# Routing stage of a two-block transformer kernel: low halves by VectorE, adaLN products elsewhere, gates behind the slots

## The chip, the cores and the metric

The kernel runs on one core of a Trainium2 chip. The metric is device time in microseconds (us). Three runs of the kernel before took 1028.23, 1029.07 and 1030.41 us; the median is 1029.07 us. Engines are named as in the profile: PE is TensorE, DVE is VectorE, ACT is ScalarE, POOL is GpSimd, SP is SyncE, whose only work here is to issue loads.

## The reference, cut to what matters

Two transformer blocks follow each other on 256 tokens of 1024 channels. The first ends in a hierarchical mixture of experts; its routing is what the change touches. `c_2` is the condition of the second block, from which that block's shifts, scales and gates are made (adaLN).

```python
# first block, after the mixer
x = x + g1 * mix
h = _rmsnorm(x, norm2_g[l]) * (1 + sc2) + sh2
g_prob = softmax(h @ rg_w + rg_b)            # 4 groups
g_p, g_idx = top_k(g_prob, 1)
e_sel = (h @ re_w + re_b)[group g_idx]       # 8 experts of the group
e_p, e_idx = top_k(softmax(e_sel), 2); e_p = e_p / sum(e_p)
gates = g_p * e_p                            # per token, two experts
y = (silu(h[tok] @ w1[e]) * (h[tok] @ w3[e])) @ w2[e]    # all 32 experts
x = x + g2 * (sum of gate * y over the token's experts)
# second block
mod = silu(c_2) @ w_ada + b_ada              # shift1, scale1, gate1, ...
```

## The kernel before

All matrices are streamed once from HBM by SP's queue into `ring`, eight buffers of 2 MB (two pools of four), in the order of `load_list`: the mixer's matrices, `wout0` and `wout1`, then the adaLN halves `ada0s`, `ada0g`, `adag1` (each two loads, `_0` and `_4`), then for each expert `w13_e_0`, `w13_e_4` and `w2_e`, 6 MB an expert. `w2_0` goes into a buffer of its own, `px`. A load is issued when its buffer's last reader is done, and SP issues strictly in its order: a load that waits holds all behind it. Which of a pool's buffers a new tile gets, and the order of instructions on each engine, is decided when the program is laid out: a scheduler takes ready instructions by priority (`tc.high_priority` raises it), and a new tile gets the buffer that comes free first in the order so laid out. `order` rows below show what it made.

Around the change the stages are these.

- Out projection (L784 to L857, `out_products`, L788): the mixer's result times `wout0` and `wout1`. Each weight tile is split into a rounded high half (ACT, L340 or L796) and the rest (DVE, L341 or L797), and three products are made. As 256 columns of x are done, DVE adds them to `x1T` (L855), PE transposes them into `tb` in PSUM (`po`, `bank`, L833) and makes the router's sums (L843), ACT squares them (L836).
- Routing (L863 to L945): the mean square gives `r2` (POOL's power, L266), DVE makes the logits `L` (L867), picks the group (L878 to L885) and the two experts (L887 to L897) and writes the selection `Mb`; PE counts ranks from it (L904 to L908), DVE makes of them the slot `rk` of each token in each expert (L910) and the selection matrix `Q` (L1023). The gates `ga` (L918 to L928) are needed only where results are put back. Beside it the rows of x are written as high and low halves `xH`, `xL` (the tiles mixH and mixL): ACT writes the high half and a full copy `xf` out of PSUM (L943, L944), POOL subtracts (L945).
- In the same place PE makes the adaLN products (`half_products`, L246): the second half of `ada0g` and both halves of `adag1`, 48 products (96 records in the profile, as each fp32 product is two). Their condition column `csl` is a copy made by POOL (L931) in a buffer of the tag `sq7`.
- Experts: `gather` (L1039) multiplies xH and xL by `Q`, `hidden` (L1056) and `outer_products` (L1087) read the streamed weights. Expert 0's products begin while its tokens are still being gathered.

Of the kernel before, what the change touches and what calls it, by code (L numbers as in the profile page):

```python
# [7 lines left out]
F32 = mybir.dt.float32  # L8
# [4 lines left out]
AF = mybir.ActivationFunctionType  # L13
OP = mybir.AluOpType
# [102 lines left out]
def build(tc, A, dbg=None):  # L117
    nc = tc.nc
# [47 lines left out]
    def yh(name, i):  # L166

        return yx.tile([128, 1032], F32R, name=name, tag=f"{name}{i}")
# [28 lines left out]
    fr = f1.enter_context(tc.tile_pool(name="fr", bufs=1))  # L197
    ptr = early.enter_context(tc.tile_pool(name="ptr", bufs=1, space=PSUM))
# [25 lines left out]
    cs = con.tile([128, 2, 8], F32, name="cs")  # L224
# [14 lines left out]
        nc.vector.tensor_copy(R, ps)  # L239
        return R  # L240

    def half_products(ps, name, cols, k0=0, k1=8):
        for k in range(k0, k1):
            w = get(f"{name}_{k // 4 * 4}")
            for j in range(4):
                nc.tensor.matmul(ps[32 * j:32 * j + 32, :], cols[:, k:k + 1].to_broadcast([128, 32]),  # L246
                                 w[:, k % 4, 256 * j:256 * j + 256], start=(k == 0), stop=(k == 7))

    def half_t(pt, R):

# [231 lines left out]
    for k in range(8):  # L482
        for j in range(4):
            nc.tensor.matmul(pss[32 * j:32 * j + 32, :], S1[:, k:k + 1].to_broadcast([128, 32]),
                             wa[:, 1 - j // 2, k, 128 * (j % 2):128 * (j % 2) + 128],
                             start=(k == 0), stop=(k == 7))
# [15 lines left out]
    for j in range(2):  # L502
        nc.scalar.activation(sg[:, j], psg[:, 256 * j:256 * j + 256], AF.Sigmoid, bias=za[:, 2 + j:3 + j])
        nc.vector.scalar_tensor_tensor(U[:, j, 30:], psv[:, 256 * j:256 * j + 256], za[:, j:j + 1], sg[:, j],
                                       op0=OP.add, op1=OP.mult)
# [9 lines left out]
    for c in range(0, 4, 2):  # L515
        ps = bank()
# [3 lines left out]
    ps = bank()  # L520
# [7 lines left out]
    for k0, k1 in ((0, 3), (3, 6), (6, 8)):  # L528
        wH, wL = w_halves(wk[:, k0:k1, 64:328])
        for a in (1, 0):  # L530
            for n, (w_, b) in enumerate(((wH, 0), (wL, 0), (wH, 1))):
                for k in range(k0, k1):
                    nc.tensor.matmul(pss[a][:, :264], hT[b][:, k, 128 * a:128 * a + 128], w_[:, k - k0],
                                     start=(n == 0 and k == 0), stop=(n == 2 and k == 7))
# [21 lines left out]
    for a in (1, 0):  # L556
# [16 lines left out]
        for n, h in enumerate([0, 2, 1, 3, 4, 6, 5, 7]):  # L573
            if n == 0:
                nc.vector.tensor_scalar(of(acc, a), rel[h], uw[:, a, h:h + 1], 0.0, op0=OP.mult, op1=OP.add)
            elif n < 7:
                nc.vector.scalar_tensor_tensor(of(acc, a), rel[h], uw[:, a, h:h + 1], of(acc, a),
                                               op0=OP.mult, op1=OP.add)
# [16 lines left out]
    for j in range(2):  # L595
        nc.vector.scalar_tensor_tensor(cqT[:, j], psq[:, 256 * j:256 * j + 256], P("qng", j), rbq,
                                       op0=OP.mult, op1=OP.mult)
# [20 lines left out]
    for j in range(2):  # L618
        ps = bank()
# [18 lines left out]
    for c in range(0, 4, 2):  # L638
        ps = bank()
# [6 lines left out]
    for c in range(0, 4, 2):  # L646
        pss = [bank(), bank()]
        for i in range(2):
            for s in range(2):
                r = slice(64 * s, 64 * s + 64)  # L650
                nc.tensor.matmul(pss[s][:, 256 * i:256 * i + 256], wuk[r, c + i, :], qT[r, c + i, :],
                                 start=True, stop=True)
# [5 lines left out]
    ps = bank()  # L658
# [30 lines left out]
    for hh in range(2):  # L689
# [3 lines left out]
        for a in (1, 0):  # L693
            S = 128 + 128 * a
            Lg[a] = fl.tile([128, 512 + 512 * a], F32, name=f"Lg{a}").rearrange("p (h t) -> p h t", h=4)
            for h in range(0, 4, 2):
                ps = bank()
# [8 lines left out]
                for j in range(h, h + 2):  # L706
                    nc.scalar.activation(Lg[a][:, j, :S], Lg[a][:, j, :S], AF.Exp, bias=nmx[:, a, j:j + 1],
                                         scale=0.125, accum_out=sm[:, a, j:j + 1])
# [32 lines left out]
    for hh in range(2):  # L741
# [15 lines left out]
        ps = bank()  # L757
        for j in range(2):
            for s in range(2):
                h = 2 * j + s  # L760
# [5 lines left out]
    def ada_rows(name, cols, ps=None, k0=0):  # L766

        ps = ps or ptr.tile([128, 512], F32, name="mod", tag="tr")[:, :256]
        half_products(ps, name, cols, k0, 8)
        R = fo.tile([128, 512], F32, name="modR")[:, :256]  # L770
        nc.scalar.activation(R, ps, AF.Copy)
        return R
# [1 line left out]
    pt = half_t(ptr.tile([128, 512], F32, name="pa", tag="tr"), ada_rows("ada0s", cs[:, 1]))  # L774
    nc.vector.tensor_add(c42(S3), pt, c42(P("ab0", 0, 8)))
    psa = ptr.tile([128, 512], F32, name="mod", tag="tr")[:, :256]
    half_products(psa, "ada0g", cs[:, 1], 0, 4)


    w0, w1 = get("wout0"), get("wout1")  # L780
# [11 lines left out]
    for c in (6, 7, 0, 1):  # L792
        for k in (0, 2):
            v = [fl.tile([128, 256], F32R, name=n, bufs=1) for n in ("weH", "weL")]
            src = (w0 if c < 4 else w1)[:, c % 4, 128 * k:128 * k + 256]
# [8 lines left out]
    rt = ms.enter_context(tc.tile_pool(name="rt", bufs=1))  # L804
# [86 lines left out]
    for a in range(2):  # L891
# [21 lines left out]
    nc.vector.tensor_reduce(cm, prk[:, 2], AX.X, OP.max)  # L913
    nc.vector.tensor_copy(ci[:, 32:33], cm)
    nc.vector.tensor_copy(ci[:, 0:32], prk[:, 2])

    ex = rt.tile([128, 2, 8], F32, name="ex")
    nc.vector.tensor_sub(ex[:, :, 0:4], L[:, :, 0:4], gm[:, :, 0:1].to_broadcast([128, 2, 4]))  # L918
# [7 lines left out]
    nc.vector.tensor_mul(oh, oh, gt[:, :, 0:2, None].to_broadcast([128, 2, 2, 32]))  # L926
    ga = rt.tile([128, 2, 32], F32, name="ga")
    nc.vector.tensor_add(ga, oh[:, :, 0], oh[:, :, 1])  # L928
    hp.__exit__(None, None, None)
    csl = fr.tile([128, 256], F32, name="csl", tag="sq7")[:, :8]  # L930
    nc.gpsimd.tensor_copy(csl, cs[:, 1])  # L931
    R_g = ada_rows("ada0g", csl, psa, 4)
    ps1 = ptr.tile([128, 512], F32, name="mod", tag="tr")[:, :256]
    half_products(ps1, "adag1", csl)

    xH, xL = ([yh(n, a)[:, :1024].rearrange("p (k t) -> p k t", k=8) for a in range(2)]
              for n in ("mixH", "mixL"))
    for b in range(2):
        for a in range(2):
            src = tb[a, b].rearrange("t (k p) -> t k p", k=4)  # L940
            h = xH[a][:, 4 * b:4 * b + 4, :]
            xf = fr.tile([128, 4, 128], F32, name="xf", bufs=2)
            nc.scalar.activation(h, src, AF.Copy, scale=r2[:, a:a + 1])  # L943
            nc.scalar.activation(xf, src, AF.Copy, scale=r2[:, a:a + 1])  # L944
            nc.gpsimd.tensor_sub(xL[a][:, 4 * b:4 * b + 4, :], xf, h)  # L945
    fs.close()

    mo = ms.enter_context(tc.tile_pool(name="mo", bufs=1))
# [142 lines left out]
    def keep(e, ps):  # L1091
        YS[e] = late[0][:, 3072 + 256 * (e % 4):3328 + 256 * (e % 4)]
        nc.scalar.activation(YS[e], ps, AF.Copy)  # L1093
# [18 lines left out]
    nc.scalar.activation(nea, B("alog"), AF.Exp)  # L1112
    nc.gpsimd.tensor_scalar(nea, nea, -1.0, None, op0=OP.mult)

    R_1 = mo.tile([128, 256], F32, name="R_1")
    nc.scalar.activation(R_1, ps1, AF.Copy)
    slots(0)
    for k in range(0, 8, 2):
        gather(0, k, 2)
    for e in range(32):  # L1120
        if e == 28:
            most = nc.values_load(ci[0:1, 32:33], min_val=0, max_val=256)
            with tc.If(most > 32):  # L1123
                off = mo.tile([128, 1], F32, name="off")
                nc.vector.memset(off, -32.0)
                with tc.For_i(0, 4, 1) as r_:
                    with tc.If(most > 32 + 64 * r_):
                        with tc.For_i(0, 32, 1) as e_:
                            own = nc.values_load(ci[0:1, bass.ds(e_, 1)], min_val=0, max_val=256)
                            with tc.If(own > 32 + 64 * r_):  # L1130
                                overflow(e_, off)
                    nc.vector.tensor_scalar(off, off, -64.0, None, op0=OP.add)
        if e % 8 == 0 and 0 < e < 24:
            slots(e // 8 + 1)
        ps = hidden(e)
        back(e)
        if e:
            scatter(e - 1)
        if e == 8:
            pt = half_t(ptr.tile([128, 512], F32, name="pa", tag="tr"), R_g)  # L1140
            nc.vector.tensor_add(c42(G3), pt, c42(P("ab0", 8, 8)))
            nc.vector.scalar_tensor_tensor(G3, G3, 1.0, P("n1w2"), op0=OP.add, op1=OP.mult)
            nc.gpsimd.tensor_mul(G3f, G3, P("fg"))
            for j in range(4):
                nc.gpsimd.tensor_mul(abG[:, :, 8 * j:8 * j + 8], abw, G3f[:, :, None].to_broadcast([128, 8, 8]))
        if e == 10:
            pt = half_t(ptr.tile([128, 512], F32, name="pa", tag="tr"), R_1)
            nc.vector.tensor_add(c42(gt1), pt, c42(P("ab1", 0, 8)))
        if e == 12:
            pb = ptr.tile([128, 256], F32, name="pb", tag="tr")  # L1150
            for k in range(8):
                nc.tensor.matmul(pb[:, 0:8], S3[:, k:k + 1].to_broadcast([128, 128]), abw[:, k],
                                 start=(k == 0), stop=(k == 7))
            nc.vector.tensor_add(abS, pb[:, 0:8], B("dtb8"))
        if e == 6:

            nc.gpsimd.dma_start(par[:, 0:NG], A["gk"])
        aT = act(e, ps)
        if e % 2 == 0 and 0 < e < 24:
            gather(e // 8 + 1, e % 8, 2)  # L1160
        if e == 0:
            first = outer_products(0, aT)
            late.append(extra[0].tile([128, 4096], F32, name="px"))
            slots(1)
            gather(1, 0, 2)
            keep(0, first)
        else:
            keep(e, outer_products(e, aT))
        pump(min(index[f"w2_{e}"] + RING, index["w2i_k"]))
# [769 lines left out]
```

## Time and profile before

| | |
|---|---|
| median of 3 runs | 1029.07 us |
| the profiled execution | 1029.3 us |
| its span | 1027.7 us |
| PE busy | 865.2 us (84%) |
| DVE, ACT, POOL busy | 440.8, 337.9, 64.3 us |
| DMA, mean over the span | 315 GB/s, 323.80 MB |
| mean granted clock of PE | 0.898 |

The page's row of transfer rates, in 40 slices of 25.7 us, reads 353, 431, 427, 426, 414, 338, 206, 416 and then 423 to 430 until slice 25. So the loads run at some 426 GB/s nearly from the start to about 642 us, but for a dent in slices 5 and 6. [...]

### The profile page before, as it was taken

The page shows a single profiled execution, that of the slowest core. Times are in us where ns is not written, and L with a number is a line of the kernel's source. Part 1 is how long each engine was busy: PE and PEld are TensorE (multiplying, and loading weights), DVE is VectorE, ACT ScalarE, POOL GpSimd, SP SyncE. Part 2 cuts the span into 40 slices and gives each one's busy share as a digit, 9 for nine tenths or more (in the row PEclk, how much of TensorE's full clock was granted, in tenths as well). Part 3 has the DMA queues.
Part 4 walks back from the last instruction along what each step waited for, and adds up shares of the span by engine and source line. Part 5 has one row for each costly group of instructions (what it writes and reads, how often), then busy time and mean ns, then how long its engine had stood idle before and what let it go on. Part 6 is the DMA issues. An engine that isn't in the chain of part 4 may idle for free. (4 is left out here: it accounts for less than half of the span.)

```text
span 1027.7 us, 19397 instructions
## 1 busy us (share of the span) xinstructions
PE 865.2 (84%) x8134; PEld 602.9 (59%) x8135; DVE 440.8 (43%) x1051; ACT 337.9 (33%) x763; POOL 64.3 (6%) x85
## 2 busy tenths in 40 slices
PE   4999998996777787667766776989999999999996
PEld 2786676653434343233332333768989878888884
DVE  1499855321101011000000104777667476666675
ACT  4441745210100010000000004745435365555562
POOL 0000002000000000000000001342012000000000
PEclk9899999997986777787778688999999999999998
DMA  9999985999999999999999999653205546444521
GB/s 353 431 427 426 414 338 206 416 423 426 427 428 423 426 428 426 424 428 427 426 426 426 424 425 425 256 213 117 104 1 233 197 166 245 165 147 182 205 83 41
DMA packets 36125, 323.80 MB, mean 315 GB/s; under 512 B 4032, under 2 KB 4416, under 8 KB 5696
## 3 DMA queue, kind: packets, MB, share of 16 engines
q1 hardware_dynamic: 34992, 320.11, 75.5%
q10 hardware_dynamic: 864, 1.86, 0.6%
q8 instruction: 66, 1.08, 0.4%
q0 software_dynamic: 176, 0.53, 0.1%
q14 instruction: 27, 0.22, 0.1%
HBM read 321.43 MB, written 1.05 MB: 314 GB/s over the span
## 5 line engine op out<-in xcount | busy, mean ns | idle before, releaser
L341 DVE TENSOR_TENSOR wL<-ring,wH 128x512 fp32r<-128x512 f32 (+1 forms) x208 | 140.1, 680 | 93.8 <-ACT wH L340 87.1
L340 ACT ACTIVATE wH<-ring 128x512 fp32r<-128x512 f32 (+1 forms) x220 | 133.9, 614 | 123.1 <-PE gb L1242 43.0
L1087 PE MATMUL yy<-ring,aT 128*32 128x256 f32 x992 | 96.6, 554 | 34.4 <-DMA ring<-w 33.7
L1075 DVE TENSOR_TENSOR at<-sl,hh 128x128 f32<-128x128 f32 x32 | 9.2, 287 | 262.3 <-ACT sl L1073 262.3
L1056 PE MATMUL hh<-ring,px 128*32 128x256 f32 x1024 | 79.1, 445 | 23.2 <-DMA ring<-w 23.2
L1056 PE MATMUL hh<-ring,XT 128*32 128x256 f32 x1024 | 71.4, 405 | 19.2 <-DMA ring<-w 19.1
L1087 PEld LDWEIGHTS yy<-ring,aT 128*32 128x32 f32 x992 | 43.1, 150 | 75.2 <-issue 55.0
L1073 ACT ACTIVATE sl<-hh 128x128 f32<-128x128 f32 x32 | 8.9, 278 | 200.5 <-PE hh L1056 189.7
L1056 PEld LDWEIGHTS hh<-ring,px 128*32 128x32 f32 x1024 | 33.0, 124 | 63.1 <-DMA ring<-w 33.4
L1093 ACT ACTIVATE px<-yy 128x256 f32<-128x256 f32 x32 | 12.3, 384 | 153.1 <-PE yy L1087 153.1
L1056 PEld LDWEIGHTS hh<-ring,XT 128*32 128x32 f32 x1024 | 32.0, 116 | 51.4 <-DMA ring<-w 27.9
L351 PE MATMUL zb<-mixH,wH 128*128 128x258 f32 x224 | 59.2, 293 | 1.2 <-ACT wH L340 1.2
L352 PE MATMUL zb<-mixH,wL 128*128 128x258 f32 x224 | 58.7, 290 | 0.0
L1242 PE MATMUL gb<-mixH,wH 128*128 128x512 f32 x176 | 54.8, 396 | 1.6 <-DVE mixH L1697 1.4
L1242 PE MATMUL gb<-mixL,wH 128*128 128x512 f32 x176 | 54.9, 394 | 0.0
L1099 PE MATMUL acc<-MT,px 32*128 32x256 f32 x512 | 43.1, 432 | 7.4 <-PEq L1123 4.3
L351 PEld LDWEIGHTS zb<-mixH,wH 128*128 128x128 f32 x224 | 43.2, 193 | 3.9 <-issue 1.6
L352 PEld LDWEIGHTS zb<-mixH,wL 128*128 128x128 f32 x224 | 43.2, 193 | 1.5 <-issue 1.5
L1099 PEld LDWEIGHTS acc<-MT,px 32*128 32x128 f32 x512 | 26.0, 200 | 26.0 <-issue 15.0
L1069 DVE COPY MT<-tm 128x256 f32<-128x256 f32 x32 | 13.6, 424 | 64.1 <-PE tm L1067 64.1
L354 PE MATMUL zb<-mixL,wH 128*128 128x258 f32 x224 | 38.7, 291 | 0.0
L1242 PEld LDWEIGHTS gb<-mixL,wH 128*128 128x128 f32 x176 | 33.0, 188 | 7.7
(550 smaller groups left out, 1648.9 us busy)
## 6 DMA issues: line engine op xcount, KB each, us to landing
ring<-w SPq DMA_DIRECT2D x132, 1024.0 KB, 22.6
ring<-wall SPq DMA_DIRECT2D x35, 2048.0 KB, 9.8
ring<-w SPq DMA_DIRECT2D x29, 2048.0 KB, 24.6
ring<-wall SPq DMA_DIRECT2D x29, 1024.0 KB, 12.9
mx<-wall SPq DMA_DIRECT2D x8, 1024.0 KB, 5.8
px<-w SPq DMA_DIRECT2D x1, 2048.0 KB, 9.3
ring<-wall SPq DMA_DIRECT2D x1, 1600.0 KB, 25.3
ring<-wall SPq DMA_DIRECT2D x1, 1536.0 KB, 25.0
```

What stands on the lines that cost most here:

```text
L340: nc.scalar.activation(d[0], src, AF.Copy)
L341: eng.tensor_sub(d[1], src, d[0])
L351: nc.tensor.matmul(ps, wH[:, k], h[0][:, q + k], start=(q + k == 0), stop=False)
L352: nc.tensor.matmul(ps, wL[:, k], h[0][:, q + k], start=False, stop=False)
L354: nc.tensor.matmul(ps, wH[:, k], h[1][:, q + k], start=False, stop=(q + k == 7))
L1056: nc.tensor.matmul(ps[32 * j:32 * j + 32], XT[e // 8][:, k, e % 8, :], w[:, k % 4, :, 128 * j:128 * j + 128], start=(k == 0), stop=(k == 7))
L1069: nc.vector.tensor_copy(MT[e], ps)
L1075: nc.vector.tensor_mul(at, sl, ps[:, 1])
L1087: nc.tensor.matmul(ps[32 * j:32 * j + 32], aT[:, 32 * c:32 * c + 32], w[:, c, 256 * j:256 * j + 256], start=(c == 0), stop=(c == 3))
L1093: nc.scalar.activation(YS[e], ps, AF.Copy)
L1099: nc.tensor.matmul(acc[j][:, i], YS[e][r, 128 * i:128 * i + 128], MT[e][r], start=(e == 0 and i == 0), stop=(e == 31), skip_group_check=True)
L1242: nc.tensor.matmul(ps.rearrange("p (x t) -> p x t", x=2), wH[:, k], y(4 * q + k), start=(q + k == 0), stop=(4 * q + k == 7), skip_group_ch ...
```

## The change

- The low halves: ACT's full copy `xf` and POOL's subtraction go. DVE makes the low half by one instruction that reads PSUM, scales it and subtracts the high half. This now stands ahead of the gates in the code.
- The block of high priority ends behind the ranks; the gates are outside it.
- `csl` has a buffer of its own. With that, nothing holds the adaLN products back to the routing.
- Of `adag1` only the first half is multiplied ahead of the experts, and copied to `R_1` by ACT; the second half is multiplied in expert 0, behind its outer products, and added by DVE.

```diff
-    def half_products(ps, name, cols, k0=0, k1=8):
+    def half_products(ps, name, cols, k0=0, k1=8, stop=True, start=True):
...
-    half_products(psa, "ada0g", cs[:, 1], 0, 4)
+    half_products(psa, "ada0g", cs[:, 1], 0, 4, False)
...
     nc.vector.tensor_copy(ci[:, 0:32], prk[:, 2])
+    hp.__exit__(None, None, None)
+
+    xH, xL = ([yh(n, a)[:, :1024].rearrange("p (k t) -> p k t", k=8) for a in range(2)]
+              for n in ("mixH", "mixL"))
+    for b in range(2):
+        for a in range(2):
+            src = tb[a, b].rearrange("t (k p) -> t k p", k=4)
+            h = xH[a][:, 4 * b:4 * b + 4, :]
+            nc.scalar.activation(h, src, AF.Copy, scale=r2[:, a:a + 1])
+            nc.vector.scalar_tensor_tensor(xL[a][:, 4 * b:4 * b + 4, :], src, r2[:, a:a + 1], h,
+                                           op0=OP.mult, op1=OP.subtract)
...
-    hp.__exit__(None, None, None)
-    csl = fr.tile([128, 256], F32, name="csl", tag="sq7")[:, :8]
+    csl = rt.tile([128, 8], F32, name="csl")
     nc.gpsimd.tensor_copy(csl, cs[:, 1])
     R_g = ada_rows("ada0g", csl, psa, 4)
     ps1 = ptr.tile([128, 512], F32, name="mod", tag="tr")[:, :256]
-    half_products(ps1, "adag1", csl)
-
...
-            xf = fr.tile([128, 4, 128], F32, name="xf", bufs=2)
-            nc.scalar.activation(h, src, AF.Copy, scale=r2[:, a:a + 1])
-            nc.scalar.activation(xf, src, AF.Copy, scale=r2[:, a:a + 1])
-            nc.gpsimd.tensor_sub(xL[a][:, 4 * b:4 * b + 4, :], xf, h)
+    half_products(ps1, "adag1", csl, 0, 4)
+    R_1 = rt.tile([128, 256], F32, name="R_1")
+    nc.scalar.activation(R_1, ps1, AF.Copy)
...
+            ps1 = ptr.tile([128, 512], F32, name="mod", tag="tr")[:, :256]
+            half_products(ps1, "adag1", csl, 4, 8)
+            nc.vector.tensor_add(R_1, R_1, ps1)
```

What the scheduler makes of it is seen at three places. On SP, the loads behind `w2_0` (px) in the kernel before; ring_2081 is `w13_0_0`, ring_2176 `w2_1`, ring_2178 and 2181 the two loads of `w13_2`, ring_2184 `w2_2`; a wait for DVE is one for the last split of wout0 or wout1, a wait for PE one for products (a wait for DMAHW is for an older load's landing):

```order
L153 DMA px_2135<-w2 128x4096 [waits DVE_49,PE_49,DMAHW7_49,Activation_49,Pool_49]
L153 DMA ring_2081<-w13 128x2048 [waits DMAHW0_49,DVE_49]
L153 DMA ring_2081<-w13 128x2048 [waits DMAHW1_49]
L153 DMA ring_2176<-w2 128x4096 [waits DMAHW2_49,DVE_49]
L153 DMA ring_2178<-w13 128x2048 [waits DMAHW3_49,PE_49]
L153 DMA ring_2178<-w13 128x2048 [waits DMAHW4_49]
L153 DMA ring_2181<-w13 128x2048 [waits DMAHW5_49,PE_49]
L153 DMA ring_2181<-w13 128x2048 [waits DMAHW6_49]
L153 DMA ring_2184<-w2 128x4096 [waits DMAHW7_49,PE_49]
L1122 TENSOR_LOAD ci_1909 [waits PE_49,DVE_49,Activation_49,Pool_49]
L1122 ISA x2
L153 DMA ring_2186<-w13 128x2048 [waits DMAHW1_49,DMAHW0_49,PE_49]
```

In the changed kernel, on the same engine and place, ring_2057 is `w13_0_0`, ring_2172 and 2175 the loads of `w13_2`, ring_2170 `w2_1`, ring_2178 `w2_2`, ring_2258, 2261 and 2180 the loads of expert 3:

```order
L153 DMA px_2111<-w2 128x4096 [waits DVE_49,PE_49,DMAHW7_49,Activation_49,Pool_49]
L153 DMA ring_2057<-w13 128x2048 [waits DMAHW0_49,PE_49]
L153 DMA ring_2172<-w13 128x2048 [waits DMAHW2_49,PE_49]
L153 DMA ring_2175<-w13 128x2048 [waits DMAHW4_49,DVE_49]
L153 DMA ring_2170<-w2 128x4096 [waits DMAHW6_49,DVE_49]
L1121 TENSOR_LOAD ci_1909 [waits PE_49,DVE_49,Activation_49,Pool_49]
L153 DMA ring_2178<-w2 128x4096 [waits DMAHW1_49,DMAHW7_49,DMAHW0_49,PE_49]
L153 DMA ring_2258<-w13 128x2048 [waits PE_49]
L153 DMA ring_2261<-w2 128x4096 [waits DMAHW2_49,PE_49]
L153 DMA ring_2180<-w13 128x2048 [waits DMAHW3_49,PE_49]
```

(The second half of each `w13` load is left out.) Before, the first load behind px waited for wout0's last split and the three after `w2_1` for adaLN products in the routing. Now the first two wait for adaLN products, which stand earlier; the next two wait for the splits of wout0 and wout1; `w2_2` goes into the buffer of `w13_0_0` itself, and its PE wait is by its count the wait for expert 0's last hidden product from that buffer. ring_2180 takes the buffer of `adag1_4`, whose products stand behind expert 0's outer products.

On PE, the adaLN products come into the out projection (po, with the split weights weH and weL, then wH and wL); one piece of the difference:

```order
 L788 MATMUL po0_1462<-mixL_936,weH_1524 128x256
 L788 MATMUL po0_1462<-mixH_934,weL_1525 128x256
+L246 MATMUL mod_1442<-ring_1939,csl_1937 32x256 x16
 L788 MATMUL po1_1463<-mixH_934,weH_1534 128x256
 L788 MATMUL po1_1463<-mixL_936,weH_1534 128x256
```

Another 16 stand in two groups of 8 a few rows below, and the 48 that stood between the router's sums (L843) and the rank counts (L904) are gone. So PE has nothing between the router's sums and the rank counts now. On DVE, one piece of the difference at the routing; mixL is the low half, goh and em lead to the choice of experts:

```order
 L878 MAX gm<-gp 128x8 x2
+L925 SCALAR_TENSOR_TENSOR mixL<-po_1643,r_1862,mixH 128x512
 L879 MAX_INDEX gi<-gm,gp 128x8 x2
-L918 TENSOR_TENSOR ex<-L,gm 128x2x4
+L929 TENSOR_TENSOR ex<-L,gm 128x2x4
+L925 SCALAR_TENSOR_TENSOR mixL<-po_1645,r_1862,mixH 128x512
 L881 CAST gidx<-gi 128x2
+L925 SCALAR_TENSOR_TENSOR mixL<-bank,r_1862,mixH 128x512 x2
 L885 TENSOR_SCALAR goh<-kon,gidx 128x4 x2
```

The four low halves stand among the choice of the group, ahead of the choice of experts. The gates (L933 to L939 now) still stand ahead of `rk` (L910) on DVE, as they did before.

## Rows read from the trace of the kernel before

**Rows 1.** Busy us by stretch: PE, PEld, DVE, ACT, POOL; then clock, DMA share, GB/s.

```profile
150.00:160.00 10.00, 10.00 (x89) 10.00 (x88) 4.97 (x13) 5.15 (x17) 0.00 (x0) 1.00 0.11 42
160.00:170.00 10.00, 8.84 (x76) 8.43 (x75) 4.84 (x12) 3.65 (x11) 0.00 (x0) 1.00 0.29 109
170.00:180.00 10.00, 6.25 (x78) 3.25 (x81) 7.59 (x31) 6.17 (x14) 5.58 (x6) 0.83 1.01 426
180.00:190.00 10.00, 9.00 (x111) 6.26 (x107) 7.33 (x24) 3.92 (x7) 1.21 (x4) 1.00 1.02 405
190.00:200.00 10.00, 9.83 (x151) 5.80 (x139) 1.77 (x6) 1.78 (x5) 0.00 (x0) 1.00 1.00 417
200.00:640.00 440.00, 321.03 (x3646) 157.83 (x3642) 51.66 (x160) 43.61 (x126) 3.42 (x7) 0.79 1.01 426
```

**Rows 2.** Waits of PE from 200 to 640 us: total us, times, longest.

```profile
PE hh L1056 <- DMA ring<-w: 42.3, 40, 2.1
PE yy L1087 <- DMA ring<-w: 33.7, 25, 2.8
```

**Rows 3.** SP's issues in order of time, three of them: start us, us.

```profile
143.28 0.33 SPq L153 DMA_DIRECT2D px<-w  x1
...
165.91 0.33 SPq L153 DMA_DIRECT2D ring<-w  x1
...
189.68 0.34 SPq L153 DMA_DIRECT2D ring<-w  x1
```

**Rows 4.** Waits of SP from 120 to 300 us, one of them.

```profile
SPq L153 <- DVE wL L341: 22.7, 2, 22.2
```

**Rows 5.** PE in order of time at the out projection, with idle time ahead.

```profile
135.05 1.93 PE L246 MATMUL mod<-ring,cs 128*32 128x256 f32 x32
...
144.41 0.39 PE L788 MATMUL po<-mixH,weH 128*128 128x256 f32 x1 [0.39 <-ACT weH L796]
...
146.37 0.39 PE L788 MATMUL po<-mixH,wH 128*128 128x256 f32 x1 [0.77 <-ACT wH L340]
```

**Rows 6.** PE in order of time at the routing.

```profile
170.09 0.53 PE L843 MATMUL bank<-rwG,x1T 128*128 128x36 f32 x4
...
176.30 5.17 PE L246 MATMUL mod<-ring,csl 128*32 128x256 f32 x64 [2.90 <-ACT modR L771]
181.40 0.19 PE L904 MATMUL side<-Mb,trib 128*128 128x32 bf16 x1
...
182.63 0.64 PE L1039 MATMUL gx<-Q,mixH 128*128 128x256 f32 x3 [0.94 <-DVE Q L1023]
```

**Rows 7.** DVE in order of time at the routing.

```profile
172.39 0.42 DVE L867 SCALAR_TENSOR_TENSOR L<-bank,r,rb 128x36 f32<-128x36 f32 x2 [0.84 <-POOL r L266]
...
173.87 2.38 DVE L885 TENSOR_SCALAR goh<-kon,gidx 128x4 f32<-128x4 f32 x2
...
177.12 1.08 DVE L919 TENSOR_TENSOR ex<-m8e 128x2 f32<-128x2 f32 x1
...
178.63 0.22 DVE L901 TENSOR_TENSOR Mb<-oh 128x64 bf16<-128x64 f32 x1
...
178.91 0.15 DVE L922 TENSOR_REDUCE gt<-ex 128x2 f32<-128x8 f32 x1
...
179.49 0.93 DVE L925 TENSOR_TENSOR gt<-gt,ex 128x2 f32<-128x2 f32 x1
180.46 0.33 DVE L926 TENSOR_TENSOR oh<-oh,gt 128x128 f32<-128x128 f32 x1
...
181.73 0.23 DVE L910 SCALAR_TENSOR_TENSOR rk<-side,Mm 128x64 f32<-128x64 f32 x1 [0.68 <-PE side L908]
```

**Rows 8.** Groups by line and shape: busy us, mean ns.

```profile
L945 POOL TENSOR_TENSOR mixL<-xf,mixH 128x512 fp32r<-128x512 f32 x4 | 5.1, 1280 | 3.0 <-ACT xf L944 2.1 <-DVE gt L922 0.9
...
L421 DVE TENSOR_TENSOR hL<-bank,hH 128x512 fp32r<-128x512 f32 x4 | 2.5, 678 | 0.0
```

**Rows 9.** A stretch of 3 us in the routing: columns as in rows 1.

```profile
176.00:179.00 3.00, 2.70 (x28) 1.33 (x32) 2.86 (x14) 1.60 (x4) 1.50 (x2) 0.50 0.95 399
```

More of the change, by code (lines that the diff above doesn't have):

```diff
@@ L246, in half_products @@
                 nc.tensor.matmul(ps[32 * j:32 * j + 32, :], cols[:, k:k + 1].to_broadcast([128, 32]),
-                                 w[:, k % 4, 256 * j:256 * j + 256], start=(k == 0), stop=(k == 7))
+                                 w[:, k % 4, 256 * j:256 * j + 256], start=start and k == k0, stop=stop and k == k1 - 1)
     def half_t(pt, R):
@@ L768, in ada_rows @@
         ps = ps or ptr.tile([128, 512], F32, name="mod", tag="tr")[:, :256]
-        half_products(ps, name, cols, k0, 8)
+        half_products(ps, name, cols, k0, 8, start=k0 == 0)
         R = fo.tile([128, 512], F32, name="modR")[:, :256]
@@ L933, in build @@
     ps1 = ptr.tile([128, 512], F32, name="mod", tag="tr")[:, :256]
-    half_products(ps1, "adag1", csl)
[L936 to L941, printed above, removed]
-            xf = fr.tile([128, 4, 128], F32, name="xf", bufs=2)
-            nc.scalar.activation(h, src, AF.Copy, scale=r2[:, a:a + 1])
-            nc.scalar.activation(xf, src, AF.Copy, scale=r2[:, a:a + 1])
-            nc.gpsimd.tensor_sub(xL[a][:, 4 * b:4 * b + 4, :], xf, h)
+    half_products(ps1, "adag1", csl, 0, 4)
+    R_1 = rt.tile([128, 256], F32, name="R_1")
+    nc.scalar.activation(R_1, ps1, AF.Copy)
     fs.close()
@@ L1113, in build @@
     nc.gpsimd.tensor_scalar(nea, nea, -1.0, None, op0=OP.mult)
-    R_1 = mo.tile([128, 256], F32, name="R_1")
-    nc.scalar.activation(R_1, ps1, AF.Copy)
     slots(0)
```

## The prediction

> **What bounds the kernel now.** I read the transfer rates first, since a kernel that streams all its weights once can be bound by them. From 200 to 640 us the DMA share is 1.01 at 426 GB/s [rows 1], and PE, with 321 of 440 us busy, waits there for loads in 65 short waits, 76 us together [rows 2]. So in the experts' stage the loads set the end. A load's delay ahead of it is paid in full at its end, and nothing there can win it back; what follows is a chain of PE and DVE work that only shifts.
>
> Next, where did the stream stand still before 200 us? It moved 0.42 MB between 150 and 160 us and 1.09 between 160 and 170 [rows 1]. By bytes its backlog ends at about 151; the 13.57 MB from 160 to 200 (the four rates times 10 us) are 31.9 us at 426 GB/s, so it runs on as if started at 168.1. That is 17 us without loads, for one reason: SP issued px at 143.28 and the next load at 165.91 [rows 3], after 22.2 us of waiting for DVE's last split of wout0 [rows 4]. From issue to the equivalent start are 2.2 us.
>
> So this change is priced by one question: when does SP issue each load, and how many has it issued when the stream last stands still? A load of 2048 KB is 2.097 MB, 4.92 us at 426 GB/s.
>
> **The loads in the new order.** The order on SP, shown with the change, puts two loads behind px whose buffers are freed by adaLN products that now run in the out projection, from some 144 us. They go out at about 146 and 150, while px is landing, and are there by 151 + 9.8 = 161. The next two wait, as before, for the splits of wout0 and wout1, at 165.91 or a little later; they are there by 180. Then `w2_2` waits for the last hidden product of expert 0 from `w13_0_0`. Before, the load with that very wait was the one issued at 189.68 [rows 3], and it cost nothing, since five loads were still landing. Now the stream is empty when it comes. So a second hole opens, between 180 and some 193 us.
>
> The sum: before, the stream restarts with an issue at 165.91 and nothing ahead. After, it restarts with an issue at T, and four loads, 4 x 4.92 = 19.7 us, lie behind it. With the same 2.2 us to get going, the stream ends later by (T - 165.91) - 19.7. What is left is T: 189.68 and all that moves expert 0.
>
> **Out projection.** 32 products (64 records) come in. 32 records took 1.93 us [rows 5], so 3.86 us. The first 16 stand where PE waited 0.39 us for ACT; from 144.41 to 146.37 PE has six products, some 0.7 us at the spacing of those records, so 1.2 us is idle [rows 5]. Taking these gaps and some shorter ones off, I set 2.0 us; the ends are 0 (all in gaps) and 3.9 (none). DVE and ACT feed PE there and move with it. The two ACT copies of 0.4 us wait on PE and lie beside its products.
>
> **Routing, from L to rk.** Before: from 172.39 to 181.73, 9.3 us [rows 7]. POOL's four subtractions, 1.28 us each [rows 8], hold DVE up: two 4-column instructions of L885 take 2.38 us, L919 1.08 [rows 7], where instructions of such size beside them take about 0.15. With POOL's work gone 2.1 + 0.9 us go. Four low halves come onto the same engine: the nearest row is a difference of the same size out of PSUM, four in 2.5 us [rows 8], so 2.5. The first exponent sum L922, now ahead of Mb, adds 0.2. Mb is thus only 0.3 us earlier. What does go is the wait behind it: the 64 records of 176.30, which end at the rank counts' 181.40 although Mb was there from about 178.8 [rows 6, 7]. But DVE has the rest of the gates in front of rk: Mm, three steps of 0.19 (178.91 to 179.49), L926, L928, some 1.5 us in all without the 0.93 of L925. rk comes 7.5 us behind L, a gain of 1.8. The ends: 4.3 (if the halves cost nothing) and a loss of 1.2 (if DVE is held up as now by something else). ACT's four full copies `xf` lay beside DVE's work; without them nothing is gained.
>
> **PE's clock.** PE now has nothing from the router's sums, which start at 170.09 [rows 6], to the rank counts. [...]
>
> **Expert 0.** The new order reads the last of `w13_0_0` four products after a gather instead of eight: 0.2 us less. Its second `adag1` half is 32 records more, 1.9 us, and one DVE add behind the outer products. Behind it stands only the first load of expert 3, ring_2180. Three loads of 14.8 us are ahead of that on the queue, which land till some 207; the products are over at about 200. Cost nothing, unless expert 0 is 5 us later than I think.
>
> T = 189.7 + 2.0 - 1.8 + 1.0 - 0.2 = 190.7. The stream ends (190.7 - 165.9) - 19.7 = 5.1 us later, and so does the kernel. Against the profiled execution (span 1027.7, 1029.3 with what lies around it) that is 1034.4; the median is 0.2 lower, so I predict 1034.2 us.
>
> With all low ends, T is 185.2 and the kernel 0.4 us faster; with all high ends 197.2 and 11.6 slower. They will not all fall on one side: some half of either way gives 1031.2 to 1037.4.
>
> **Rivals.**
>
> - No change that can be told (within 0.2%, about 2 us): T falls between 183.6 and 187.6. The gain in routing must be 3 to 7 us larger. For it: PE's 5.17 us leave the path. Against: DVE, not PE, is then the one that rk waits for. The sum is zero at T = 185.6, which gives 1029.1; chance 0.11.
> - Faster: the two loads that are brought forward are the whole gain. This holds if `w2_2` is not held, so that the stream restarts at about 168 with the wout splits and stays full: 165.9 + 2.0 - 9.8 against 165.9, 7.8 us less, 1021.3. It decides from T = 177.5 down; between that and 183.6 the gain is smaller. Against: the gather itself began only at 182.63 [rows 6], and no reading of w13_0_0 is possible before. It could come true only if the buffer that `w2_2` waits for were another than its count says. Chance, with smaller gains, 0.08.
> - Slower by more: expert 0 runs late (cold clock through the gather, halves dearer out of PSUM), the stream also waits for `adag1_4`'s buffer behind expert 0's outer products. From T of about 195 on its products end too late for the 207 us above, and the load of ring_2180 is late as well; with T = 195 to 197 the sum gives 9.4 to 11.4 us, 1038.5 to 1040.5. Chance 0.06.
> - The change does not do what it says: the gates stay ahead of rk on DVE, as the order shows. This is in the sum already (1.5 us); were they behind, T would be some 0.8 us earlier.
>
> **How the numbers follow.** The forecast, 1031.2 to 1038, has 0.75, and all of it is slower by over 0.2%, which is about what a measurement here can tell. With the slow rival slower has 0.81, same 0.11, faster 0.08. The range 1030.5 to 1038.0 takes in the forecast and the upper edge of "no change"; it leaves out the faster cases, the rest of "no change" and the slow rival, some 0.2.
>
> **What would show it.** In rates of the changed kernel: 426 GB/s on to about 161 us, a first hole to about 169, a second from about 180 to 193, then full to about 645. On SP: two loads between 145 and 151, two near 168, `w2_2` at 190.7. On DVE: L885 near 0.3 us for two, four new instructions of some 0.65 us, rk 7.5 us behind L. On PE: the clock at 0.50 when the gather starts. I am wrong if there is no second hole, or if the stream is not full behind it.

## The result and the profile after

The changed kernel takes 1034.16 us (median of 6 runs, 1033.82 to 1036.17); the kernel before, beside it, 1028.65. The ratio is 1.0057, 95% interval 1.0044 to 1.0069: slower by 5.5 us. The profiled execution has a span of 1033.0 us, before 1027.7. The forecast was 1034.2. Two executions of the later runs, one of the kernel before (1058.37 us) and one of a variant (3252.80 us), went at a far lower mean granted clock (0.796 and 0.234) and are left out of all medians, ratios and intervals here.

The transfer rates of the changed kernel, as in [rows 1] (busy us of PE, PEld, DVE, ACT, POOL, then PE's granted clock as a share of its full speed, DMA share, GB/s):

```profile
150.00:160.00 10.00, 10.00 (x89) 10.00 (x88) 5.06 (x12) 4.75 (x14) 0.00 (x0) 1.00 0.99 407
160.00:170.00 10.00, 9.42 (x82) 9.22 (x80) 4.55 (x11) 4.88 (x15) 0.00 (x0) 1.00 0.18 66
170.00:180.00 10.00, 1.67 (x15) 1.45 (x14) 7.01 (x34) 4.08 (x10) 1.53 (x4) 0.73 0.89 375
180.00:190.00 10.00, 8.33 (x57) 6.39 (x57) 6.25 (x24) 2.68 (x5) 0.00 (x0) 0.59 0.01 2
190.00:200.00 10.00, 9.28 (x141) 5.78 (x144) 1.87 (x5) 1.50 (x4) 0.00 (x0) 1.00 0.74 279
200.00:640.00 440.00, 322.22 (x3701) 158.67 (x3693) 50.18 (x155) 40.85 (x122) 1.24 (x5) 0.80 1.01 426
```

The one hole of before has become two: 66 GB/s where the wout loads are waited for, and 2 GB/s from 180 to 190. From 200 us on the rate is 426 GB/s in both kernels, so nothing is won back. That the whole difference is a stream that ends later is seen at its end. The stretch from 640 to 720 us, first of the kernel before, then of the changed one:

```profile
640.00:720.00 80.00, 73.85 (x900) 61.96 (x901) 62.06 (x127) 44.40 (x101) 30.21 (x27) 0.96 0.53 200
```

```profile
640.00:720.00 80.00, 70.78 (x842) 57.85 (x840) 61.08 (x131) 45.65 (x104) 32.66 (x28) 0.96 0.61 229
```

29 GB/s more over 80 us are 2.3 MB that were still to come, 5.4 us at 426 GB/s.

SP's issues in the changed kernel (start us, us; beside [rows 3]):

```profile
142.61 0.33 SPq L153 DMA_DIRECT2D px<-w  x1
145.28 0.90 SPq L153 DMA_DIRECT2D ring<-w  x2
...
148.84 0.81 SPq L153 DMA_DIRECT2D ring<-w  x2
167.50 0.33 SPq L153 DMA_DIRECT2D ring<-w  x1
168.25 1.09 SPq L153 DMA_DIRECT2D ring<-w  x2
191.54 0.34 SPq L153 DMA_DIRECT2D ring<-w  x1
```

Two loads go out early, two behind the splits of wout (a load of w13 is two issues, one of w2 is one), and the next at T = 191.54. SP's waits from 120 to 300 us have the one for T in the first of these rows (total us, times, longest); the second answers to [rows 4]:

```profile
SPq L153 <- PE hh L1057: 18.6, 6, 8.3
SPq L153 <- DVE wL L341: 18.0, 2, 17.8
SPq L1121 <- DVE ci L914: 12.8, 1, 12.8
```

The third row is a wait that the prediction does not have: ahead of this load SP reads `ci`, the counts of the routing, and waits for them until 182. The wait for the hidden products follows it and ends last, so it is the one that sets T.

PE in order of time, beside [rows 5] and [rows 6]:

```profile
143.28 1.93 PE L246 MATMUL mod<-ring,csl 128*32 128x256 f32 x32
...
171.72 0.53 PE L843 MATMUL bank<-rwG,x1T 128*128 128x36 f32 x4
...
180.02 0.18 PE L904 MATMUL side<-Mb,trib 128*128 128x32 bf16 x1 [7.76 <-DVE Mb L901]
...
181.97 0.98 PE L1040 MATMUL gx<-Q,mixH 128*128 128x256 f32 x3 [1.65 <-DVE Q L1024]
...
190.84 1.50 PE L1057 MATMUL hh<-ring,XT 128*32 128x256 f32 x24
```

DVE in order of time, beside [rows 7]:

```profile
174.03 0.42 DVE L867 SCALAR_TENSOR_TENSOR L<-bank,r,rb 128x36 f32<-128x36 f32 x2 [0.83 <-POOL r L266]
174.84 0.73 DVE L925 SCALAR_TENSOR_TENSOR mixL<-po,r,mixH 128x512 fp32r<-128x512 f32 x1
...
177.88 0.35 DVE L885 TENSOR_SCALAR goh<-kon,gidx 128x4 f32<-128x4 f32 x2
...
179.74 0.22 DVE L901 TENSOR_TENSOR Mb<-oh 128x64 bf16<-128x64 f32 x1
...
181.08 0.22 DVE L910 SCALAR_TENSOR_TENSOR rk<-side,Mm 128x64 f32<-128x64 f32 x1
```

From L to rk are 7.05 us where 9.34 were [rows 7]; PE stood idle for 7.76 us up to the rank counts. And the clock, a stretch of the routing and gather beside [rows 9]:

```profile
175.00:188.00 13.00, 6.33 (x35) 5.11 (x35) 10.60 (x47) 4.27 (x8) 0.15 (x1) 0.50 0.29 124
```

The gather and the first hidden products run at the lower level, 0.50, until 188. From the gather's start to T are 9.57 us; before, at clock 1.00, 7.05 [rows 3, 6].

### The profile page after: what moved, and what is told of

It is laid out like the page before. It is cut to its first block, busy times and chain, and to the rows that moved or that the text cites. A ratio compares the mean times of both kernels' runs of the same rounds, so it can differ in the third digit from the quotient of the medians.

```text
span 1033.0 us, 19392 instructions
## 1 busy us (share of the span) xinstructions
PE 863.8 (84%) x8134; PEld 602.8 (58%) x8135; DVE 440.0 (43%) x1056; ACT 335.4 (32%) x759; POOL 59.4 (6%) x81
## 5 line engine op out<-in xcount | busy, mean ns | idle before, releaser
L1088 PE MATMUL yy<-ring,aT 128*32 128x256 f32 x992 | 94.1, 541 | 35.8 <-DMA ring<-w 35.4
```

The costliest lines, as they stand in the source:

```text
L1088: nc.tensor.matmul(ps[32 * j:32 * j + 32], aT[:, 32 * c:32 * c + 32], w[:, c, 256 * j:256 * j + 256], start=(c == 0), stop=(c == 3))
```

## Experiments

The theory is the prediction's: the kernel ends later by (T - 165.9) - 4.92 x n, T being the issue of the load that waits for expert 0's first buffer and n the loads ahead of it. This holds where the stream stands still when T comes; where it still runs, the hole before is the last one and sets the end. The main rival: something in routing itself (the low halves out of PSUM, the gates) costs the time. Diffs are against the changed kernel.

**The halves alone.** All adaLN products go back to the routing; the low halves by DVE and the gates' place stay.

```diff
-    csl = rt.tile([128, 8], F32, name="csl")
+    csl = fr.tile([128, 256], F32, name="csl", tag="sq7")[:, :8]
...
-    half_products(ps1, "adag1", csl, 0, 4)
+    half_products(ps1, "adag1", csl)
```

> The changed kernel with the adaLN products back in the routing, all 48 of them, and their buffers freed there; low halves on DVE and the gates' place stay. Theory of the holes (the end is set by when the stream of loads last restarts and how many loads lie behind that): one hole, from 151 to the wout splits at 166, five loads of 4.9 us land until 191, expert 0 frees the next buffer at 189 to 190.5, so no second hole; within 0.8 us of before, ratio 0.999 to 1.001. Rival, that the low halves on DVE or the gates cost the time: 4 to 6 us slower than before, ratio 1.004 to 1.006. Rival, that the shorter routing pays by itself: 1 to 2 us faster.

Measured: 1029.93 us, before 1029.34, ratio 0.9998 (0.9988 to 1.0007). L to rk takes 7.15 us. PE and the issues:

```profile
175.16 3.66 PE L246 MATMUL mod<-ring,csl 128*32 128x256 f32 x64 [1.74 <-ACT modR L771]
178.75 0.19 PE L904 MATMUL side<-Mb,trib 128*128 128x32 bf16 x1
180.44 0.63 PE L1038 MATMUL gx<-Q,mixH 128*128 128x256 f32 x3 [1.40 <-DVE Q L1022]
```

```profile
165.93 0.33 SPq L153 DMA_DIRECT2D ring<-w  x1
...
187.53 0.82 SPq L153 DMA_DIRECT2D ring<-w  x2
```

The buffer comes free 2.15 us earlier than before, and the time is the same: five loads behind 165.93 still land then (437 GB/s from 180 to 190 us). So with the low halves on DVE routing is shorter, they cost no time, and with one hole the shorter routing buys none.

**The adaLN products alone.** Low halves and gates as before; the products as in the changed kernel.

```diff
-            nc.vector.scalar_tensor_tensor(xL[a][:, 4 * b:4 * b + 4, :], src, r2[:, a:a + 1], h, ...)
+            nc.scalar.activation(xf, src, AF.Copy, scale=r2[:, a:a + 1])
+            nc.gpsimd.tensor_sub(xL[a][:, 4 * b:4 * b + 4, :], xf, h)
```

> The kernel before with the adaLN part of the change alone: csl in its own buffer, half of adag1 in expert 0; low halves by ACT and POOL, gates at high priority. Theory of the holes: two holes, four loads ahead of the second, expert 0 frees the next buffer at 191 to 193; 5 to 7 us slower than before, ratio 1.005 to 1.007. Rival, that the halves on DVE are what costs: ratio 0.999 to 1.002.

Measured: 1036.07, ratio 1.0064 (1.0050 to 1.0078). DVE and PE:

```profile
176.24 2.38 DVE L885 TENSOR_SCALAR goh<-kon,gidx 128x4 f32<-128x4 f32 x2
```

```profile
182.73 0.21 PE L904 MATMUL side<-Mb,trib 128*128 128x32 bf16 x1 [9.74 <-POOL trib L811]
```

Two holes again, T = 193.62. The loss is there with this part alone. L885 is back at 2.38 us: POOL's subtractions make the difference to 0.35. The rank counts wait 2 us past Mb (180.72) for `trib`, a cast that stands behind the subtractions on POOL, so T is 2.1 us later than in the changed kernel (0.7 of it because px is later in this execution).

**The second half of adag1 in routing.** It runs behind the router's sums instead of in expert 0, so that its buffer is free before the gather and n is 5.

```diff
+    csm = fr.tile([128, 256], F32, name="csm", tag="sq7")[:, :8]
+    nc.gpsimd.tensor_copy(csm, cs[:, 1])
+    half_products(ps2, "adag1", csm, 4, 8)
...
-            half_products(ps1, "adag1", csl, 4, 8)
```

> The changed kernel, but the second half of adag1 is multiplied in the routing, ahead of the rank counts, not in expert 0: its buffer comes free at about 175 and w2_2 takes it. Theory of the holes: five loads of 4.92 us lie ahead of the second hole, not four; with expert 0's first buffer free at 191 to 192 the end is 0.5 to 1.5 us later than before, so 4 to 5 us faster than the changed kernel; ratio to before 1.0005 to 1.0015. Rival, that PE's and DVE's path through the routing sets the end: as the changed kernel, ratio 1.005 to 1.006.

Measured: 1030.12, before 1029.34, ratio 1.0006 (0.9997 to 1.0015). SP:

```profile
168.03 1.75 SPq L153 DMA_DIRECT2D ring<-w  x3
175.62 0.33 SPq L153 DMA_DIRECT2D ring<-w  x1
190.98 0.81 SPq L153 DMA_DIRECT2D ring<-w  x2
```

T is within 0.6 us of the changed kernel's: the gather starts 0.86 us later (182.83), but the clock is back at 1.00 within 185 to 186 instead of at 188, and from the gather to T are 8.15 us. The time is 4.7 us below that of the changed kernel; T accounts for 0.6 of it, so the issue at 175.62 takes back some 4 of the 5.5 us. This is the run that decides for the count of loads.

**TensorE kept at work.** 24, then 11 products that nobody reads, between the sums and the rank counts (the second diff has 11 for 24).

```diff
+    for i in range(24):
+        nc.tensor.matmul(wps, r2[:, 0:1].to_broadcast([128, 128]), x1T[:, i % 8], start=True, stop=True)
```

> The changed kernel with 24 products of no use (x1T by r2, into a spare PSUM tile that nobody reads) on PE between the router's sums and the rank counts, about 5 us of work in the 7.8 us in which PE waits there. Theory that the low clock at the gather is 2 to 2.5 us of the loss: clock 1.00 from 182 on, expert 0 frees its first buffer at 189 to 189.5 instead of 191.5, so 2 to 2.5 us faster than the changed kernel, ratio to before 1.003 to 1.0035. Rival, that DVE and ACT set the pace of the gather whatever the clock: no faster than the changed kernel, 1.005 to 1.006.

Measured: 1037.79, ratio 1.0081 (1.0067 to 1.0095), outside both the expectation and its rival: 24 products were put at about 5 us and took 12.31. PE:

```profile
174.75 12.31 PE L949 MATMUL warmps<-x1T,r 128*128 128x256 f32 x48 [1.79 <-POOL r L266]
186.90 0.18 PE L904 MATMUL side<-Mb,trib 128*128 128x32 bf16 x1
188.11 0.63 PE L1043 MATMUL gx<-Q,mixH 128*128 128x256 f32 x3 [0.93 <-DVE Q L1027]
```

The rank counts came 6.9 us late, but T (195.20) only 3.7: from the gather to T are 7.09 us at clock 1.00.

> The changed kernel with 11 products added whose result nobody reads, behind the router's sums and ahead of the rank counts on TensorE. In e4_warm 24 such products took 12.3 us from 174.75, held the rank counts up by 6.9 us, and the gather behind them ran at granted clock 1.00 (7.09 us from its start to the gated load T instead of 9.57). Eleven end by about 180, where the rank counts started anyway. Theory (T alone sets the end, and the cold clock of the gather is 2.5 us of T): T = 189.0 to 189.5, the kernel 2 to 2.5 us faster than the changed one, about 1031.9, ratio to before 1.003. Rival (the clock through the gather is set by something else, or falls again in the 2 us between the rank counts and the gather): T = 191.5, time 1034.2, ratio 1.0055. Second rival (the products again hold the rank counts): T = 193 or more, ratio above 1.007.

Measured: 1033.35, before 1029.48, ratio 1.0035 (1.0022 to 1.0048). PE, and the clock:

```profile
174.24 6.70 PE L949 MATMUL warmps<-x1T,r 128*128 128x256 f32 x22 [1.79 <-POOL r L266]
180.78 0.18 PE L904 MATMUL side<-Mb,trib 128*128 128x32 bf16 x1
...
182.16 0.63 PE L1043 MATMUL gx<-Q,mixH 128*128 128x256 f32 x3 [1.10 <-DVE Q L1027]
```

```profile
175.00:176.00 1.00, 1.00 (x3) 0.74 (x3) 1.00 (x8) 1.00 (x3) 0.35 (x1) 0.50 0.86 360
176.00:178.00 2.00, 2.00 (x6) 1.64 (x5) 2.00 (x6) 0.65 (x2) 0.00 (x0) 0.50 1.09 459
178.00:179.00 1.00, 1.00 (x5) 0.83 (x5) 0.93 (x7) 0.00 (x0) 0.00 (x0) 0.88 0.84 360
```

The low clock now falls on products that nobody waits for, and is over ahead of the gather: T = 189.24, 7.08 us behind its start and 2.3 us earlier than in the changed kernel. The ratio falls by 0.0022, which is 2.3 us too; by the medians it is 1.6, and the two intervals touch, so it is the trace and not the time that shows the size.

**Gates behind rk.** The steps from the product of the sums on are made to read rk.

```diff
+    nc.vector.scalar_tensor_tensor(gz, rk[:, :, 0:1], 0.0, gt[:, :, 0:1], op0=OP.mult, op1=OP.add)
```

> The changed kernel with the rest of the gates (from the product of the exponent sums on) made to read rk, so that VectorE can run them only behind rk. The prediction put these steps at 1.5 us in front of rk, of which 0.8 us would show. The trace since then shows the rank counts starting at 180.02 and rk at 181.08, so TensorE's counts are likely what rk waits for next. Theory: rk 0.4 us earlier, T = 191.1, time 0.4 us below the changed kernel, 1033.8, not to be told from it; ratio to before 1.005. Rival (the gates are the whole of the delay): T = 190.0, ratio 1.004. Other rival (behind rk they hold up the slots and expert 0): T = 192 or later, ratio 1.006 or more.

Measured: 1034.51, ratio 1.0049 (1.0033 to 1.0064), not to be told from the changed kernel. DVE:

```profile
180.51 0.22 DVE L901 TENSOR_TENSOR Mb<-oh 128x64 bf16<-128x64 f32 x1
181.12 0.23 DVE L910 SCALAR_TENSOR_TENSOR rk<-side,Mm 128x64 f32<-128x64 f32 x1 [0.25 <-PE side L908]
```

rk comes 0.61 us behind Mb instead of 1.34, and now waits for PE: 0.7 us, close to the prediction's 0.8. T is 190.89, though px is 0.81 later in this execution; besides the gates, the clock was back within 186 to 187, and from the gather to T are 8.80 us.

**Both repairs.** All of `adag1` in the routing as PE's work there, only ada0g's half early; then the same with the gates behind rk.

```diff
-    half_products(ps1, "adag1", csl, 0, 4)
+    csm = fr.tile([128, 256], F32, name="csm", tag="sq7")[:, :8]
+    nc.gpsimd.tensor_copy(csm, cs[:, 1])
+    half_products(ps1, "adag1", csm)
```

> The changed kernel with the products of adag1 all in routing, behind the router's sums (64 records, as TensorE's work between the sums and the rank counts), and only the second half of ada0g in the out projection. Five loads lie ahead of the gated one, one of them early, and TensorE has work until shortly before the rank counts. By e1_halves_alone: rk 7.15 us behind L, T 7.1 us behind the gather's start at clock 1.00. L comes 1 us later than in that run (32 records in the out projection), so gather 181.4, T = 188.5. Theory of the holes: end shift (188.5 - 165.9) - 5 x 4.92 = -2.0 us, time 1026.7, ratio to before 0.998, faster than both kernels. Rival (as in e1_halves_alone an earlier T buys nothing, and the restart behind the splits of wout sets the end): 1029 to 1030, ratio 1.000 to 1.001.

> e7_whole_adag1_in_gap and e6_gates_behind together. Theory: a further 0.4 us of T, T = 188.1, time 1026.3, ratio to before 0.9975; not to be told from e7 by the time, only by rk in the trace. Rival (gates behind rk hold up the slots): T later than in e7 and the time above it.

Measured: 1028.46, ratio 0.9988 (0.9979 to 0.9997), and 1026.67, ratio 0.9977 (0.9968 to 0.9985); before 1029.48 beside both. The second is the fastest version, 2.4 us under the kernel before by the ratio and 2.8 by the medians. By the time the second came out as expected; the first fell 1 us short, between the expectation (0.998) and its rival (1.000). In both profiles T is 1.5 us or more later than expected, at 189.98 and 189.79; that of the second is of one of its three slowest executions (1028.19 us, beside eight of 1026.1 to 1026.9). PE, first of the one, then of the other:

```profile
172.75 5.35 PE L246 MATMUL mod<-ring,csm 128*32 128x256 f32 x64 [0.85 <-POOL csm L945]
179.67 0.18 PE L904 MATMUL side<-Mb,trib 128*128 128x32 bf16 x1 [1.57 <-DVE Mb L901]
```

```profile
172.44 3.66 PE L246 MATMUL mod<-ring,csm 128*32 128x256 f32 x64 [0.85 <-POOL csm L947]
179.36 0.18 PE L904 MATMUL side<-Mb,trib 128*128 128x32 bf16 x1 [3.26 <-DVE Mb L901]
...
180.66 0.98 PE L1042 MATMUL gx<-Q,mixH 128*128 128x256 f32 x3 [1.01 <-ACT R L1119]
```

PE has its work done early and waits again, 1.57 and 3.26 us ahead of the rank counts. The clock went to 0.50 in the first again at 183, in the gather, and in the second at 179.5, ahead of it. The gates' part is seen from L to the gather: 7.93 us in the first, 7.29 in the second.

**Filling the rest.** Eight products ahead of adag1's and four behind the rank counts; then the eight alone.

```diff
+    for i in range(8):
+        nc.tensor.matmul(wp0, r2[:, 0:1].to_broadcast([128, 128]), x1T[:, i % 8], start=True, stop=True)
     prk = side()[:, :96].rearrange("p (n e) -> p n e", n=3)
```

> e8_whole_and_gates with 12 products added whose result nobody reads: 8 between the router's sums and adag1's products, 4 between the rank counts and the gather. In e8 TensorE stood idle for 3.26 us ahead of the rank counts and 1.01 ahead of the gather, and the granted clock was 0.50 from 179.5 to 187, so that the gated load was issued 9.13 us behind the gather's start; at clock 1.00 it was 7.08 in e5_short_warm. 8 products are 2.1 us at full clock and end, with adag1's 3.7 us, about 179, ahead of the rank counts. Theory: T = 189.8 - 2.0 = 187.8, end shift (187.8 - 165.9) - 24.6 = -2.7 us by the sum, where e8 by the same sum had -0.7 and -2.4 in its times: 2 us faster than e8, about 1024.8, ratio to before 0.9958. Rival (the clock falls all the same, as it did in e7 while TensorE was at work): T = 190 or later by the products, ratio 0.998 or above. Rival (the other hole, behind the wout splits, now binds): not below ratio 0.9965.

> e9_filled without the 4 products behind the rank counts. Theory: TensorE has only the 1.0 us ahead of the gather without work, as e5_short_warm had 1.10 with the clock at 1.00 through it, so T and the time are those of e9, ratio 0.996. Rival: the last microsecond matters, the clock is 0.50 in the gather, T 2 us later than in e9 and ratio 0.998.

Measured: 1031.95, ratio 1.0021 (1.0005 to 1.0037), and 1027.81, ratio 1.0003 (0.9988 to 1.0017); before 1029.23. The executions of both fall into two groups (twelve of the first: 1028.0 to 1030.7 and 1033.2 to 1034.7; eleven of the second: 1025.4 to 1027.8 and 1030.0 to 1032.6), so their medians say little. The second's PE:

```profile
172.79 3.72 PE L905 MATMUL warm<-x1T,r 128*128 128x256 f32 x16 [1.79 <-POOL r L266]
176.57 3.66 PE L246 MATMUL mod<-ring,csm 128*32 128x256 f32 x64
180.16 0.19 PE L907 MATMUL side<-Mb,trib 128*128 128x32 bf16 x1
...
184.77 0.64 PE L1062 MATMUL hh<-ring,XT 128*32 128x256 f32 x8 [0.39 <-DVE XT L1052]
```

A miss, by the price: eight products are 3.7 us at full clock, not 2.1, so they hold the rank counts up past Mb (178.49). In the first the clock was down as well (0.50 from 174 to 176), they took 5.14 us, and the counts came at 182.69. The clock in the gather was 1.00 in both, as intended, but the products added for it had held the rank counts up: T is 193.35 and 189.42. In the second a further cost shows: from the gather (181.46) to T are 7.96 us at clock 1.00, not 7.09, as PE waits for XT, which DVE writes behind the gates there. So in this profile the gates behind rk take back about what they gave.

All runs against the sum (n loads ahead of T; time is the median less that of before beside it):

| kernel | T | n | sum, us | span - 1027.7 | time, us |
|---|---|---|---|---|---|
| changed | 191.54 | 4 | +5.9 | +5.3 | +5.5 |
| adaLN alone | 193.62 | 4 | +8.0 | +10.3 | +6.7 |
| second half in routing | 190.98 | 5 | +0.5 | -0.9 | +0.8 |
| 24 products | 195.20 | 4 | +9.6 | +9.4 | +8.5 |
| 11 products | 189.24 | 4 | +3.6 | +3.1 | +3.9 |
| gates behind rk | 190.89 | 4 | +5.3 | +4.2 | +5.0 |
| whole adag1 in routing | 189.98 | 5 | -0.5 | -0.2 | -1.0 |
| the same, and gates | 189.79 | 5 | -0.7 | -1.1 | -2.8 |
| 8 and 4 products | 193.35 | 5 | +2.8 | +1.4 | +2.7 |
| 8 products | 189.42 | 5 | -1.1 | -2.2 | -1.4 |

The halves alone are not in the table: at their T of 187.53 the stream still runs, so the sum gives 0; the span was 0.8 us shorter, the time 0.6 longer. The sum ranks the kernels but for neighbours, and is within 1.5 us of all spans but one. That one, adaLN alone, was profiled in its slowest execution (1039.68 us; the other four took 1035.25 to 1036.68).

How much the clock takes is seen in the six profiles in which it was 0.50 in the gather. How long it lay there is an estimate from the clock of slices of half a us; 7.08 us is the stretch at clock 1.00.

| kernel | clock 0.50 from the gather to T, us | gather to T, us | lost for each us at 0.50 |
|---|---|---|---|
| changed | 6.2 | 9.57 | 0.40 |
| adaLN alone | 5.5 | 9.30 | 0.40 |
| the whole adag1, and gates | 5.2 | 9.13 | 0.39 |
| gates behind rk | 4.5 | 8.80 | 0.38 |
| whole adag1 in routing | 3.4 | 8.37 | 0.38 |
| second half in routing | 3.0 | 8.15 | 0.36 |

Executions of one kernel differ by some 2 to 7 us, the two kernels with 8 products most. Where the clock falls may differ between them, as it did between the two versions with adag1 in routing: of the 8 and 4 products, the five fastest executions have a mean granted clock of 0.911 to 0.916, the six slowest 0.904 to 0.911. With one profile of each kernel that is not shown, and why the clock fell where it did stays open, as does most of the last column's distance from the sum.

## Why the prediction was right, point by point

- **The loads set the end, and a hole is paid in full.** Right: 5.4 us by bytes, 5.5 by time.
- **A second hole, gated by expert 0.** Right. It was foreseen for 180 to 193 and lay there. The first half of the proof is the halves alone (shorter routing, no change), the second the one more load ahead, which took back some 4 of the 5.5 us.
- **T.** Forecast 190.7, measured 191.54. Out projection: L is 1.64 us later, and px in this execution 0.67 earlier, so 2.3 against 2.0. Routing: 9.34 to 7.05, 2.3 us gained against 1.8; the halves took 0.74 each against 0.65, and L885 went to 0.35 as foreseen. Gates ahead of rk: 0.7 against 0.8, by the run that puts them behind.
- **The clock was the mis-sized term.** It stands in the sum for T with 1.0 us (ends 0 and 2.6), less 0.2 for the order. That 1.0 was my estimate, and no run shows it; from the gather to T the runs show 2.5 us (9.57 at 0.50 for 6.2 us of it, 7.05 before at 1.00). The 0.2 did not show: with the new order at clock 1.00 the stretch is 7.08 and 7.09 us, before 7.05. I had taken the 1.3 us that 64 records lost at 0.50 (5.17 us [rows 6, 9], where twice the 1.93 of 32 records is 3.86 [rows 5]) as nearly the whole, and set part of that aside as hidden beside DVE and ACT. But the gather and the hidden products of the first buffer are a chain that PE leads, 7.05 us long at full clock, and it met the low clock for 6 us.
- **Why the number fits all the same.** The clock's term was 1.7 us too small, the gain in routing 0.5 too small, and L came 0.4 earlier than forecast in this execution, so T was 0.8 late; and the span shifted by 5.3 us where this T gives 5.9 by the sum. The forecast added 5.1 us to a median of 1029.07; beside the changed kernel the kernel before took 1028.65, and the change was 5.5. The mechanism was right; that the median came within 0.1 us is luck, these errors standing against each other.
- **Rivals.** "No change" needed T between 183.6 and 187.6; no run with the early products came below 189. "Faster" needed the gated load not to be held; it was, for 8.3 us. It had a further obstacle that the prediction left out: SP's read of `ci`, ahead of that load, ended only at 183.1, for which the sum gives 2.4 us faster at best, not 7.8. The slow rival began at T = 195, which only the 24 products reached, where the sum still held.
- **Small slips in the sums.** "Faster" at its full size begins at T = 177.8, not 177.5, and half of the way to the low ends is about 1031.4, not 1031.2. Nothing hangs on either.

POOL's hold on DVE was measured by undoing it: L885 is 2.38 us with the four subtractions (before, and the adaLN products alone) and 0.35 in all kernels without. In the kernel before, it ends with two subtractions that began 0.13 us ahead of it (176.25 and 176.23, [rows 7]):

```profile
173.74 2.49 POOL L945 TENSOR_TENSOR mixL<-xf,mixH 128x512 fp32r<-128x512 f32 x2 [1.38 <-ACT xf L944]
```

DVE's two 4-column instructions lasted 2.38 us beside the 2.49 of POOL's two. By what means POOL holds DVE, no run here shows.

## What to carry to other kernels

Where loads are the bound, price a change by the stream: for each stand-still find the instruction that the next load waits for, and count the loads already ahead of it. Bringing a load forward by leaving another buffer occupied trades one load for a hole; moving the other half of the same products 25 us earlier was worth 4.7 us here, the routing shortened by 2.2 us alone nothing. And when work is taken off PE, look at what runs next on it: here, behind 7.76 us without work, the gather met a clock of 0.50, and it stood on the path to T, 2.5 us longer than before.

## What the runs showed of the hardware

- PE's granted clock fell to 0.50 after it had stopped: in the changed kernel within 174 to 175, behind sums that ended at 172.3. It came back only in the gather, at 188, after 9.7 us without work except for the rank counts, and 6 us of work. In the kernel with 11 products it was 0.50 from 175 on although PE had been at work again since 174.24, and rose within 178 to 179. The same 64 records of adag1 behind the same sums took 5.35 us in one version (clock 0.50 from 173 to 176) and 3.66 in the other (1.00 from 172 to 179).
- A stretch of gather and hidden products, in which PE, DVE and ACT take turns, lost 0.36 to 0.40 us for each us that it ran at 0.50 (estimates from six profiles).
- A product of 128x128 by 256 fp32 columns whose weights are a column broadcast cost 0.46 us at clock 1.00 (8 products, 16 records, in 3.72 us). I had expected 0.26, read from the counts of records in slices of 1 us, in which a record that spans a boundary stands in both slices.
